# Retention over a prompt of 512 frames: one pass over all pairs of blocks, or blocks of 128 frames joined by carried states

## The chip, the core and the metric

The kernel runs on one core of a Trainium2 chip. A core has a matrix engine (TensorE, in the profile PE, its weight loads PEld), a vector engine (VectorE, DVE), a scalar engine (ScalarE, ACT), a general engine (GpSimd, POOL) and a queue engine (SyncE, SP), which run side by side and wait for each other by semaphores. DMA queues are fed here by SP (loads) and POOL (stores). The metric is the time of one execution on the device in microseconds, as the median of several runs.

## The reference

One inference step of an encoder layer with weights shared by a prompt (one sequence of 512 frames) and eight sample streams of 16 frames, at width 1024. The layer has a half-step feed-forward block, a mixer, a second feed-forward block and a per-layer embedding. The mixer projects the normed input once into all its parts and runs two token mixers: forgetting attention (FoX, 8 heads) and retention (4 heads with keys of 128 and values of 256). The part that matters here is the retention:

```python
def step(state, qkv):
    qc, kc, vc = ...                      # one chunk of 64 frames
    inter = einsum('bchk,bhkv->bchv', qc, state) * inter_decay
    att = einsum('bihk,bjhk->bhij', qc, kc) * intra_decay[None]
    intra = einsum('bhij,bjhv->bihv', att, vc)
    new_state = state * chunk_decay + einsum('bjhk,bjhv->bhkv', kc * kv_decay, vc)
    return new_state, (inter + intra)
```

Inside a chunk of 64 frames every frame sees every other, with decay gamma to the power |t - s|; earlier chunks are seen with decay gamma to the power (t - s), later ones not at all. The four heads have gamma = 1 - 2^-5 to 1 - 2^-8. The final state of the prompt and of the samples are outputs too. After the retention come an RMS norm of each head, a gate silu(rg) and a projection.

## The kernel before

All tokens stand in one axis of T = 640 columns: the prompt's 512 (S) and the samples' 128. Channels lie on the 128 partitions. Large products are made in fp32r with operands split into two parts (`wh`, `wl` of the weights; a high and a low part of x), three matmuls for one. The small products of attention and retention are plain fp32 matmuls, which show in the profile as two passes each.

The stage of interest is in the middle. The input projection is a list of units (`units`, from line 1552 on), each a weight load, splits of the weights, some 50 to 100 matmuls and a take of the result. They are run by a generator, `feed`. The retention's work is woven into it by hand: after each step of a head, `fill(FILL_R)` lets the feed issue matmuls worth 2.45 us by a planned clock (`clock`, counted up in `mm`). A scheduler that simulates the engines then orders each engine's instructions by this order and by when their operands are ready, so it can pull feed matmuls ahead or push a step back. After the last head `drain` issues what is left of the feed. What follows is the retention's output projection, whose operand is read back from `retd`.

A head (`Retention`, line 1325) goes through thirteen steps before the change:

- `rotate(0)`, `rotate(1)`: rotary embedding of k and q (DVE), from tiles loaded out of `zdram` by `first_loads` and `loads`.
- `scores(0)` to `scores(3)`: keys of block j (128 frames) against all queries from block j on, so 512, 384, 256 and 128 columns. Each goes to a PSUM bank of its own, and DVE multiplies it with the mask row of the head (`self.mask`, 128 x 512, loaded for each head into an `att` buffer), giving four `att` tiles. `scores(4)` is the samples' part.
- `values(0)`, `values(1)`: for each half of the 256 value channels, four matmuls of 512, 384, 256 and 128 columns added up in one bank, copied out by ACT. `square` squares them; `values_s` does the samples.
- `flip`: the keys transposed by PE; DVE scales each of the four blocks with the decay to the end of the prompt (`kd`), and the samples' block twice (`kb`).
- `sizes` (mean squares and their inverse roots, a row of small DVE instructions) and `gates` (two loads from `zdram`, silu on ACT).
- `state_p`: four matmuls of 256 columns add up the prompt's final state in one bank; ACT copies it and POOL stores it.
- `finish`: the norm's factors are spread by PE, DVE multiplies, POOL stores two tiles to `retd`.
- `states`: the samples' states, in four banks, added by DVE, stored by POOL (1 MB).

The next head's loads are issued at fixed steps: `first_loads` (k, q) at step 3, `loads` (the rest, v and the mask) at step 9, `more_loads` (the samples' state) at step 13. Three of a head's tiles (k and q; q's turned half with v; the samples' state) are taken in turn from four `kv` buffers, so a head's k and q go into the buffer of the state of two heads earlier, once that is stored. The `att` tag has 8 buffers, the `pa` tag 6 PSUM banks.

Line 205 is the matmul in `mm`, line 228 the transpose, lines 282 and 283 the split of weights; lines 816 to 834 take the results of feed units, line 1531 those of the FoX projection, which is the last of the feed.

Of the kernel before, what the change touches and what calls it, by code (L numbers as in the profile page):

```python
# [14 lines left out]
ALU = mybir.AluOpType  # L15
# [4 lines left out]
P = 128  # L20
D = 1024
KC = D // P
S = 512
NB = 8
# [26 lines left out]
for _name, _n in (  # L51
    ("ident", 128), ("triu", 128), ("trib", 128), ("tris", 128), ("causal", 128), ("bd", 128),
    ("sel8", 128), ("fold", 64), ("lmask", 16), ("cmask", 16), ("bsel", 8), ("kd", 16), ("ksd", 8),
):
    SM[_name] = (_at, _at + _n)
    _at += _n
# [7 lines left out]
def shape_constants():  # L64
# [25 lines left out]
    kd = np.zeros((P, RH, S // P))  # L90
    ksd = np.zeros((P, RH, 2))
    for h in range(RH):
        for t in range(S // P):
            kd[:, h, t] = gam[h] ** (S - 1 - (t * P + i)) * scale
        for j in range(2):
            ksd[:, h, j] = np.where(b % 2 == j, gam[h] ** (L - 1.0 - l) * scale, 0.0)
    put("kd", kd.reshape(P, -1))
    put("ksd", ksd.reshape(P, -1))

    q = np.arange(S)  # L100
    rmask = np.zeros((RH, P, S))
    smask = np.zeros((P, RH, P))
    gq = np.zeros((P, RH, 2, 2 * L))
    for h in range(RH):
        dist = q[None, :] - i[:, None]
        same = (q[None, :] // CHUNK) == (i[:, None] // CHUNK)
# [25 lines left out]
def kernel(  # L132
# [1192 lines left out]
    class Retention:  # L1325
# [33 lines left out]
        def scores(self, j):  # L1359
            kr, qr = self.z[0][0], self.z[1][0]  # L1360
            if j == 0:
                self.ats = []
            ps = bank()
            if j < 4:
                n = S - j * P
                mm(ps[:, :n], kr[:, j * P:(j + 1) * P], qr[:, j * P:S], True, True)
                at = att()
                nc.vector.tensor_tensor(at[:, :n], ps[:, :n], self.mask[:, :n], op=ALU.mult)
                self.ats.append(at)
            else:  # L1370
                mm(ps[:, :P], kr[:, S:], qr[:, S:], True, True)
                self.at_s, self.qg = tmp([P, P]), tmp([P, NB // 2, 2, 2 * L])
                nc.vector.tensor_tensor(self.at_s, ps[:, :P], smt[:, self.hd, :], op=ALU.mult)
                qp = qr[:, S:].rearrange("p (r m) -> p r m", r=NB // 2).unsqueeze(2).to_broadcast([P, NB // 2, 2, 2 * L])
                gp = gqt[:, self.hd].unsqueeze(1).to_broadcast([P, NB // 2, 2, 2 * L])
                nc.vector.tensor_tensor(self.qg, qp, gp, op=ALU.mult)

        def values(self, dvb):
# [4 lines left out]
            for j in range(4):  # L1383
                mm(po[:, j * P:S], self.vs[j][:, dsl], self.ats[j][:, :S - j * P], j == 0, j == 3)
# [32 lines left out]
        def flip(self):  # L1417
# [5 lines left out]
            for t in range(4):  # L1423
                nc.vector.tensor_scalar(self.kd[:, t, :], pk[:, t * P:(t + 1) * P], cs["kd"][:, hd * 4 + t:hd * 4 + t + 1], None, op0=ALU.mult)
# [24 lines left out]

        def state_p(self):  # L1450
            ps = bank()
            for t in range(4):
                mm(ps[:, :DV], self.kd[:, t, :], self.vs[t], t == 0, t == 3)
            sf = tmp([P, DV])
            nc.scalar.copy(sf, ps[:, :DV])
            nc.gpsimd.dma_start(o_state_p[0, 0, self.hd], sf)
# [167 lines left out]
    load(smt, c_smask)  # L1624
    heads = [Retention(hd) for hd in range(RH)]
# [144 lines left out]
```

## Time and profile before

| what | value |
|---|---|
| median of 3 runs (lowest, highest) | 1656.47 us (1654.16, 1657.26) |
| the profiled execution | 1657.02 us |
| its span, first to last instruction | 1655.3 us |
| granted TensorE clock, share of full speed | 0.999 |
| DMA, mean over the span | 150 GB/s, 248.66 MB |

A row of a view that groups instructions reads: line, engine, operation, tile written <- tiles read, shapes, count, then busy time in us, mean ns of one, and the idle time of the engine before them with what ended it. A row of a timeline reads: start in us, length in us, engine, line, operation, tiles, shapes and how many in a row. The view of stretches gives, for each stretch, each engine's busy time in us, the granted clock, the busy share of the DMA engines and GB/s. A wait "PE pa L205 <- DVE blk L1447: 1.9, 1, 1.9" says that matmuls into `pa` waited for that DVE line 1.9 us in all, once, at most 1.9.

### The profile page before, as it was taken

The numbers are of one execution on the slowest core, as the hardware profiler recorded it, in microseconds if no ns is written. First come the engines' busy times: TensorE is split into PE (matmuls) and PEld (weight loads), VectorE is DVE, ScalarE is ACT, GpSimd is POOL, SyncE is SP. The second block draws the span as 40 slices with busy tenths as digits, with TensorE's granted clock in tenths as the row PEclk, the third lists the DMA queues.
The fourth block names the chain that finished last, engine by engine and source line by source line (L and its number), as shares of the span: only waits on it lengthen the run. The fifth ranks groups of instructions, "written<-read, shape, count | busy, mean of one in ns | idle before, by whom it ended". The sixth has DMA issues, their size and how long they took to land.

```text
span 1655.3 us, 30447 instructions
## 1 busy us (share of the span) xinstructions
PE 1638.0 (99%) x12019; PEld 1562.2 (94%) x12019; DVE 1164.5 (70%) x2480; ACT 737.0 (45%) x1522; POOL 99.2 (6%) x180
## 2 busy tenths in 40 slices
PE   8999999999999999999999999999999999999998
PEld 8999999999999888888789988999999999999998
DVE  6884787586876646666688876658885687568663
ACT  6552344244454445344444345435553355235432
POOL 0000000000111111000001020001000000000000
PEclk9999999999999999999999999999999999999999
DMA  8244233433623225576765687634334424332531
GB/s 244 77 138 145 87 92 119 154 85 108 212 77 117 96 103 179 211 268 231 279 214 188 205 292 247 216 109 156 97 96 155 132 77 134 132 116 87 171 120 46
DMA packets 207647, 248.66 MB, mean 150 GB/s; under 512 B 10464, under 2 KB 176272, under 8 KB 203408
## 3 DMA queue, kind: packets, MB, share of 16 engines
q1 hardware_dynamic: 195264, 203.22, 38.4%
q0 software_dynamic: 12032, 43.42, 7.1%
q8 instruction: 94, 1.54, 0.4%
q14 instruction: 49, 0.40, 0.1%
q10 hardware_dynamic: 208, 0.08, 0.0%
HBM read 198.04 MB, written 48.65 MB: 149 GB/s over the span
## 4 chain that ended last, share of the span: by engine, by line
PE 84%; issue 9%; DMA 4%; DVE 2%; POOL 1%; ACT 1%; SPq 1%; POOLq 0%; DVEq 0%; ACTq 0%
PE pa L205 67%; PE pg L205 14%; PE pa L228 3%; DMA raw<-in_ffn_w_in_dram 2%; DMA blk<-zdram 1%; DVE wl L283 0%; DMA out_dram<-kv 0%; POOL zdram L832 0%; PE pg L228 0%; POOL zdram L835 0%; DMA kv<-in_x_prompt_dram 0%; SPq L650 0%; DMA kv<-zdram 0%; DVE raw L424 0%; DVE blk L283 0%
## 5 line engine op out<-in xcount | busy, mean ns | idle before, releaser
L282 ACT CAST wh<-raw 128x512 fp32r<-128x512 f32 (+1 forms) x525 | 316.1, 613 | 489.3 <-PE pa L205 296.8
L205 PE MATMUL pa<-blk,wh 128*128 128x320 f32 x2344 | 511.3, 311 | 2.9 <-ACT wh L282 1.0
L283 DVE TENSOR_TENSOR wl<-raw,wh 128x512 fp32r<-128x512 f32 (+1 forms) x525 | 351.8, 678 | 96.6 <-ACT wh L282 92.9
L205 PEld LDWEIGHTS pa<-blk,wh 128*128 128x128 f32 x2344 | 387.3, 188 | 10.9 <-ACT wh L282 2.4
L205 PE MATMUL pa<-blk,wl 128*128 128x320 f32 x1172 | 342.6, 308 | 0.0
L205 PE MATMUL pa<-kv,wh 128*128 128x320 f32 x1344 | 251.7, 308 | 0.0
L205 PEld LDWEIGHTS pa<-blk,wl 128*128 128x128 f32 x1172 | 215.4, 188 | 0.1
L205 PEld LDWEIGHTS pa<-kv,wh 128*128 128x128 f32 x1344 | 210.7, 188 | 0.0
L205 PE MATMUL pg<-blk,wh 128*128 128x320 f32 x768 | 177.0, 317 | 4.2 <-DVE pg L822 1.6
L205 PE MATMUL pa<-blk,blk 128*128 128x320 f32 (+2 forms) x1064 | 168.8, 304 | 0.0
L205 PE MATMUL pa<-kv,wl 128*128 128x320 f32 x672 | 154.6, 308 | 0.0
L205 PEld LDWEIGHTS pa<-blk,blk 128*128 128x128 f32 (+1 forms) x1064 | 151.8, 183 | 2.1 <-PE pa L205 1.2
L205 PE MATMUL pg<-wh,blk 128*128 128x256 f32 x768 | 148.2, 286 | 0.0
L205 PEld LDWEIGHTS pg<-blk,wh 128*128 128x128 f32 x768 | 127.4, 188 | 10.1 <-issue 2.5
L205 PEld LDWEIGHTS pg<-wh,blk 128*128 128x128 f32 x768 | 120.8, 188 | 6.1 <-issue 4.8
L205 PE MATMUL pg<-blk,wl 128*128 128x320 f32 x384 | 118.9, 310 | 0.0
L205 PEld LDWEIGHTS pa<-kv,wl 128*128 128x128 f32 x672 | 112.7, 188 | 0.0
L205 PE MATMUL pg<-wl,blk 128*128 128x256 f32 x384 | 108.4, 283 | 0.0
L283 DVE TENSOR_TENSOR blk<-raw,blk 128x512 fp32r<-128x512 f32 x82 | 56.3, 688 | 50.0 <-ACT blk L282 37.2
L282 ACT CAST blk<-raw 128x512 fp32r<-128x512 f32 x82 | 50.7, 621 | 79.2 <-DMA raw<-in_ffn_w_in_dram 65.6
L205 PE MATMUL pa<-wh,blk 128*128 128x256 f32 (+1 forms) x432 | 82.6, 285 | 0.0
L205 PEld LDWEIGHTS pg<-wl,blk 128*128 128x128 f32 x384 | 72.1, 188 | 1.7 <-issue 1.1
(289 smaller groups left out, 2247.7 us busy)
## 6 DMA issues: line engine op xcount, KB each, us to landing
raw<-in_ffn_w_in_dram SPq DMA_DIRECT2D x86, 512.0 KB, 5.2
raw<-in_w_in_mix_dram SPq DMA_DIRECT2D x25, 1024.0 KB, 5.5
raw<-in_ffn_w_out_dram SPq DMA_DIRECT2D x16, 1024.0 KB, 5.4
kv<-in_cache_fox_k_dram SPq DMA_DIRECT2D x16, 1024.0 KB, 6.4
kv<-in_cache_fox_v_dram SPq DMA_DIRECT2D x16, 1024.0 KB, 6.7
blk<-xd SPq DMA_DIRECT2D x48, 320.0 KB, 6.0
xd<-blk POOLq DMA_DIRECT2D x40, 320.0 KB, 3.2
zdram<-blk POOLq DMA_DIRECT2D x32, 320.0 KB, 2.8
```

Source lines behind the costliest of these rows:

```text
L205: i = nc.tensor.matmul(out, lhsT, rhs, start=start, stop=stop, **kw)
L228: tick(nc.tensor.transpose(out, in_, ident[: in_.shape[0], : in_.shape[0]]), 0.11)
L282: nc.scalar.copy(hi, src)
L283: nc.vector.tensor_tensor(lo, src, hi, op=ALU.subtract)
```

## The change

The four blocks of 128 frames become chunks of their own. Each block's scores are made against its own queries alone (four matmuls of 128 columns into one bank), masked by one DVE multiply with a 128 x 128 mask that all blocks share. The state behind each block is made before the values: `kd` now decays to the end of the block, one factor for all blocks, and `states_p` forms state t = state t-1 x gamma^128 + product of block t on DVE; two products share a bank. The last of these states is the prompt's final state and is stored from there, so `state_p` is gone. The queries of blocks 1 to 3 are scaled by gamma^(i+1) (`qd`), and `values` adds, for these blocks, state t-1 times `qd` to the product within the block.

The masks of all heads are two tiles of 128 x 512 (`masks`: within a block, and gamma^(i+1)), loaded once ahead of the heads into `att` buffers that stay taken. The steps are put in a new order, twelve for a head: `flip` third, then `scores`, `scores_s`, `states_p`, the values, `sizes` and `gates`, `states`, `finish`. The next head's `first_loads` are still at step 3, `loads` at step 6, `more_loads` at step 11. `FILL_R` stays 2.45.

```diff
-    rmask = np.zeros((RH, P, S))
+    rmask = np.zeros((2, P, RH, P))
...
-        rmask[h] = np.where(same | (dist >= 0), gam[h] ** np.abs(dist), 0.0) * scale
+        rmask[0, :, h] = np.where(same | (dist >= 0), gam[h] ** np.abs(dist), 0.0) * scale
+        rmask[1, :, h] = gam[h] ** (i[None, :] + 1.0)
...
-            self.mask = blk([P, S], tag="att")
-            load(self.mask, c_rmask[hd], 40.0)
...
-        def scores(self, j):
+        def scores(self):
...
+            for t in range(4):
+                sl = slice(t * P, (t + 1) * P)
+                mm(ps[:, sl], kr[:, sl], qr[:, sl], True, True)
+            self.at = att(shape=(P, 4, P))
+            within = masks[0][:, self.hd].unsqueeze(1).to_broadcast([P, 4, P])
+            nc.vector.tensor_tensor(self.at, ps.rearrange("p (t q) -> p t q", t=4), within, op=ALU.mult)
+            self.qd = att(shape=(P, 3, P))
+            fall = masks[1][:, self.hd].unsqueeze(1).to_broadcast([P, 3, P])
+            nc.vector.tensor_tensor(self.qd, qr[:, P:S].rearrange("p (t q) -> p t q", t=3), fall, op=ALU.mult)
...
+        def states_p(self):
+
+            held = [att(shape=(P, 2, DV)) for _ in range(2)]
+            self.behind = [held[t // 2][:, t % 2, :] for t in range(4)]
+            for u in range(2):
+                ps = bank()
+                for t in (2 * u, 2 * u + 1):
+                    new, st = ps[:, (t % 2) * DV:(t % 2 + 1) * DV], self.behind[t]
+                    mm(new, self.kd[:, t, :], self.vs[t], True, True)
+                    if t == 0:
+                        nc.vector.tensor_copy(st, new)
+                    else:
+                        nc.vector.scalar_tensor_tensor(st, self.behind[t - 1], gam[self.hd] ** P, new, op0=ALU.mult, op1=ALU.add)
+            nc.gpsimd.dma_start(o_state_p[0, 0, self.hd], self.behind[3])
...
-            for j in range(4):
-                mm(po[:, j * P:S], self.vs[j][:, dsl], self.ats[j][:, :S - j * P], j == 0, j == 3)
+            for t in range(4):
+                mm(po[:, t * P:(t + 1) * P], self.vs[t][:, dsl], self.at[:, t, :], True, t == 0, skip_group_check=True)
+                if t > 0:
+                    mm(po[:, t * P:(t + 1) * P], self.behind[t - 1][:, dsl], self.qd[:, t - 1, :], False, True, skip_group_check=True)
...
-            for t in range(4):
-                nc.vector.tensor_scalar(self.kd[:, t, :], pk[:, t * P:(t + 1) * P], cs["kd"][:, hd * 4 + t:hd * 4 + t + 1], None, op0=ALU.mult)
+            nc.vector.tensor_scalar(self.kd, pk.rearrange("p (t k) -> p t k", t=4), cs["kd"][:, hd:hd + 1], None, op0=ALU.mult)
...
-        def state_p(self):
-            ps = bank()
-            for t in range(4):
-                mm(ps[:, :DV], self.kd[:, t, :], self.vs[t], t == 0, t == 3)
-            sf = tmp([P, DV])
-            nc.scalar.copy(sf, ps[:, :DV])
-            nc.gpsimd.dma_start(o_state_p[0, 0, self.hd], sf)
...
+    masks = [att(shape=(P, RH, P)) for _ in range(2)]
+    for n in range(2):
+        load(masks[n], c_rmask[n])
...
-            lambda: r.rotate(0), lambda: r.rotate(1), lambda: (r.scores(0), heads[hd + 1].first_loads() if hd + 1 < RH else None),
-            lambda: (r.scores(1), r.scores(2)),
-            lambda: (r.scores(3), r.scores(4)), lambda: r.values(0), lambda: (r.values(1), r.square()), lambda: r.values_s(),
-            lambda: (r.flip(), heads[hd + 1].loads() if hd + 1 < RH else None),
-            lambda: (r.sizes(), until(("rg", hd)), r.gates()), lambda: r.state_p(), lambda: r.finish(),
-            lambda: (r.states(), heads[hd + 1].more_loads() if hd + 1 < RH else None),
+            lambda: r.rotate(0), lambda: r.rotate(1), lambda: (r.flip(), heads[hd + 1].first_loads() if hd + 1 < RH else None),
+            lambda: r.scores(), lambda: r.scores_s(),
+            lambda: (r.states_p(), heads[hd + 1].loads() if hd + 1 < RH else None),
+            lambda: r.values(0), lambda: (r.values(1), r.square()), lambda: r.values_s(),
+            lambda: (r.sizes(), until(("rg", hd)), r.gates()),
+            lambda: (r.states(), heads[hd + 1].more_loads() if hd + 1 < RH else None), lambda: r.finish(),
```

More of the change, by code (lines that the diff above doesn't have):

```diff
@@ L89, in shape_constants @@
     scale = DK ** -0.5
-    kd = np.zeros((P, RH, S // P))
+    kd = np.zeros((P, RH))
     ksd = np.zeros((P, RH, 2))
     for h in range(RH):
-        for t in range(S // P):
-            kd[:, h, t] = gam[h] ** (S - 1 - (t * P + i)) * scale
+        kd[:, h] = gam[h] ** (P - 1.0 - i) * scale
         for j in range(2):
             ksd[:, h, j] = np.where(b % 2 == j, gam[h] ** (L - 1.0 - l) * scale, 0.0)
-    put("kd", kd.reshape(P, -1))
+    put("kd", kd)
     put("ksd", ksd.reshape(P, -1))
-    q = np.arange(S)
-    rmask = np.zeros((RH, P, S))
+    rmask = np.zeros((2, P, RH, P))
     smask = np.zeros((P, RH, P))
@@ new lines, in scores_s @@
+        def scores_s(self):
+            kr, qr = self.z[0][0], self.z[1][0]
+            ps = bank()
+            mm(ps[:, :P], kr[:, S:], qr[:, S:], True, True)
+            self.at_s, self.qg = tmp([P, P]), tmp([P, NB // 2, 2, 2 * L])
+            nc.vector.tensor_tensor(self.at_s, ps[:, :P], smt[:, self.hd, :], op=ALU.mult)
+            qp = qr[:, S:].rearrange("p (r m) -> p r m", r=NB // 2).unsqueeze(2).to_broadcast([P, NB // 2, 2, 2 * L])
+            gp = gqt[:, self.hd].unsqueeze(1).to_broadcast([P, NB // 2, 2, 2 * L])
+            nc.vector.tensor_tensor(self.qg, qp, gp, op=ALU.mult)
@@ new lines, in states_p @@
+        def states_p(self):
+            held = [att(shape=(P, 2, DV)) for _ in range(2)]
+            self.behind = [held[t // 2][:, t % 2, :] for t in range(4)]
+            for u in range(2):
+                ps = bank()
+                for t in (2 * u, 2 * u + 1):
[6 more added lines that the diff above has]
+            nc.gpsimd.dma_start(o_state_p[0, 0, self.hd], self.behind[3])
```

21 lines of the change are left out of this document (3 added, 18 removed).

## The prediction

> **What bounds the kernel now.** I read the page first, for the engine that is busy and for the chain that ended last, then stretches of the four heads, then what ended the waits in them.
>
> ```profile
> span 1655.3 us, 30447 instructions
> PE 1638.0 (99%) x12019; PEld 1562.2 (94%) x12019; DVE 1164.5 (70%) x2480; ACT 737.0 (45%) x1522; POOL 99.2 (6%) x180
> PE 84%; issue 9%; DMA 4%; DVE 2%; POOL 1%; ACT 1%; SPq 1%; POOLq 0%; DVEq 0%; ACTq 0%
> ```
>
> TensorE is busy for 99% of the span and is 84% of the chain. A microsecond of its work taken away is a microsecond of time, unless PE then waits for something. What could be waited for is read from the stage itself. The next fence is the table of stretches from each head's first score matmul to the next head's, and then the list of waits of PE over the same time.
>
> ```profile
> core 0: us, PE busy (x) PEld busy (x) DVE busy (x) ACT busy (x) POOL busy (x), PEclk, DMA share, GB/s
> 853.00:907.00 54.00, 54.00 (x362) 49.41 (x361) 47.53 (x103) 22.40 (x42) 5.50 (x11) 1.00 0.49 158
> 907.00:957.00 50.00, 49.31 (x330) 44.56 (x329) 42.97 (x97) 19.86 (x40) 5.16 (x9) 1.00 0.65 215
> 957.00:999.00 42.00, 38.49 (x267) 33.83 (x265) 28.38 (x72) 20.94 (x48) 8.52 (x15) 1.00 0.91 316
> 999.00:1039.00 40.00, 38.09 (x244) 32.76 (x245) 26.88 (x66) 23.48 (x36) 3.62 (x6) 1.00 0.68 234
> ```
>
> ```profile
> PE pa L205 <- DVE blk L1447: 1.9, 1, 1.9
> PE pg L205 <- DVE pg L822: 1.6, 1, 1.6
> PE pg L205 <- DVE blk L1531: 1.6, 1, 1.6
> PE pg L205 <- DVE blk L831: 0.7, 1, 0.7
> ```
>
> Two things are to be seen. In heads 0 and 1 PE never or hardly stops, but VectorE (DVE) is busy 47.53 of 54 and 42.97 of 50 us, 88% and 86%. In heads 2 and 3 PE stands still for 3.5 and 1.9 us, and all but 0.3 of the stage's 6.1 us of PE waits are ended by DVE. So PE sets the pace of this stage and DVE is the next in line. The DMA share reaches 0.91 in head 2.
>
> **The matmuls removed (the main term).** An fp32 matmul appears as two passes. Pieces in a timeline overlap at their ends, so I measure from one start to a later start and take off the fp32r feed matmuls in between. These are head 0's scores, its values (both halves of the channels), and eight passes of 128 columns in its finish:
>
> ```profile
> 852.81 2.32 PE L205 MATMUL pa<-kv 128*128 128x512 f32 x8
> 854.88 0.54 PE L205 MATMUL pg<-blk,wh 128*128 128x320 f32 x2
> 855.26 0.31 PE L205 MATMUL pg<-blk,wl 128*128 128x320 f32 x1
> 855.40 0.45 PE L205 MATMUL pg<-blk,wh 128*128 128x320 f32 x2
> 855.70 0.31 PE L205 MATMUL pg<-blk,wl 128*128 128x320 f32 x1
> ...
> 860.46 1.66 PE L205 MATMUL pa<-att,kv 128*128 128x512 f32 x4
> 861.66 0.75 PE L205 MATMUL pa<-blk,wh 128*128 128x320 f32 x2
> 862.25 2.97 PE L205 MATMUL pa<-att,kv 128*128 128x256 f32 x12
> 864.98 0.54 PE L205 MATMUL pg<-blk,wh 128*128 128x320 f32 x2
> 865.35 0.31 PE L205 MATMUL pg<-blk,wl 128*128 128x320 f32 x1
> ...
> 900.16 1.05 PE L205 MATMUL pa<-sm,ty 128*128 128x128 f32 x8
> 900.97 0.54 PE L205 MATMUL pg<-blk,wh 128*128 128x320 f32 x2
> 901.35 0.31 PE L205 MATMUL pg<-blk,wl 128*128 128x320 f32 x1
> ```
>
> - A feed matmul: three from 855.26 to 855.70, so 0.147 us.
> - Scores before: 852.81 to 855.26 is 2.45 us, less two feed matmuls 2.16 us. They stream 512 + 384 + 256 + 128 = 1280 columns in two passes.
> - Values before: 860.46 to 865.35 is 4.89 us, less four feed matmuls 4.30 us, twice the scores, as it must be.
> - A pass of 128 columns: 900.16 to 901.35 is 1.19 us, less two feed matmuls 0.90 us for eight, so 0.112 us each.
> - Scores after: 4 matmuls of 128 columns, 8 passes, 0.90 us. Values after: (4 + 3) matmuls for each of two halves, 28 passes, 3.14 us.
>
> Before 6.46, after 4.04 us: 2.42 us less in a head, **9.7 us in four heads**. The state's matmuls (`kd` against `vs`, four of 256 columns) keep number and shape; they only stop accumulating in one region. The sample's parts, the transposes and the finish are unchanged on PE.
>
> **VectorE and ScalarE.** DVE rows for the shapes removed and for the nearest ones to those added:
>
> ```profile
> L1368 DVE TENSOR_TENSOR att<-pa,att 128x512 f32<-128x512 f32 (+3 forms) x16 | 7.0, 480 | 0.0
> L1424 DVE TENSOR_SCALAR att<-pa,sm 128x128 f32<-128x128 f32 x16 | 4.6, 342 | 0.0
> L1468 DVE SCALAR_TENSOR_TENSOR kv<-kv,pa 128x512 f32<-128x512 f32 x16 | 10.1, 679 | 0.5 <-PE pa L205 0.5
> L1301 DVE COPY att<-pa 128x512 f32<-128x512 f32 x8 | 5.5, 685 | 0.6 <-PE pa L228 0.5
> L1445 DVE TENSOR_TENSOR blk<-blk,blk 128x512 f32<-128x512 f32 x8 | 5.4, 686 | 5.3 <-ACT blk L1434 5.3
> L1376 DVE TENSOR_TENSOR tmp<-kv,tmp 128x256 f32<-128x256 f32 x4 | 1.6, 412 | 0.0
> ...
> L1455 ACT COPY tmp<-pa 128x256 f32<-128x256 f32 x4 | 1.5, 364 | 0.7 <-PE pa L205 0.7
> ```
>
> Removed in a head: 4 x 480 + 4 x 342 ns = 3.29 us of DVE and one ACT copy of 0.36 us. Added: one masked multiply of 512 columns, 0.68 (as L1445; L1376 already reads broadcast operands, at no visible cost); `qd`, 384 columns, halfway between 412 and 686, 0.55; `kd` in one go, at least 0.69 (L1301), at most the 1.37 of today, taken as 342 plus 384 columns at the 1.07 ns a column between L1376 and L1445, 0.75; a copy of 256 columns, 685 - 274 = 0.41; three decay-and-add of 256 columns, 679 - 274 each, 1.22. Together 3.61 us: **0.3 us more DVE in a head, 1.3 us in all**. PE loses 2.4 us of own work in a head, and one step with its 2.45 us of feed moves out of each head (12 steps, not 13). On head 1's row, DVE then carries about 43.0 + 0.3 less the feed's share (2.45 x 0.86 = 2.1), 41.2 us, over 50 - 4.9 = 45 us: 91%. Since DVE ends nearly all of PE's waits here, I charge its 1.3 us in full, as time given back. Its other end is nothing, if the load still hides under PE.
>
> **Moves and queues.** `flip` goes from step 9 to step 3, so `kd` is ready three steps ahead of its use, and the kv buffer that holds k and q of this head comes free for the next head's second load (now issued at step 6, not 9). `states` goes ahead of `finish`, so the sample's state store leaves POOL's queue one step sooner, ahead of the two `retd` stores. That matters, because this chain of waits stands in the trace:
>
> ```profile
> 957.08 5.97 DMA out_dram<-kv
> ...
> 963.07 3.09 DMA kv<-zdram
> ...
> 966.28 0.09 DVE kv L1355
> ```
>
> Head 3's k and q wait for the store of head 1's state, DVE waits for them at the head of its queue, and PE for the DVE instruction behind (the 1.6 us at L822). Earlier stores and loads can shorten this; a shorter head brings the need for them earlier by about as much. I take nothing for it. The bound on the good side is all 6.1 us of PE's waits.
>
> The mask loads are these, one of 256 KB in each head:
>
> ```profile
> att<-in_c_rmask_dram SPq DMA_DIRECT2D x4, 256.0 KB, 7.3
> ```
>
> ```profile
> 825.56 7.14 SPq L214 DMA_DIRECT2D kv<-zdram  x6
> ```
>
> They become two, both ahead of head 0's loads in the program, so 512 KB less is moved. The two tiles stay in two of the 8 `att` buffers, but a head now takes 5 more and not 6. Queued on SP they can delay head 0's loads by about an issue each; the second row shows those loads going out from 825.56 us on, and head 0's scores come at 852.81, so I take nothing.
>
> At the end, 4 x 2.45 = 9.8 us of planned feed are left behind the last head, which `drain` then issues. Today feed and head 3 end together, so this remainder covers head 3's way through `retd` and back:
>
> ```profile
> 1036.63 1.96 PE pg L205 x12
> 1038.59 6.53 PE pa L205 x48
> ```
>
> **The sum.** -9.7 + 1.3 = -8.4 us against the profiled execution, 1657.0 us with its span of 1655.3. The median of the three runs shown is 1656.5, 0.5 lower; there the sum gives 1648.1, and I say **1648 us**.
>
> **Rivals.**
> - *The stage's waits go too.* The earlier state stores and loads end the waits of heads 2 and 3. Up to 6.1 us more, without the DVE charge: 1656.5 - 9.7 - 6.1 = 1640.7. For it: each wait there hangs on a late load or a late head. Against: loads fall due earlier too.
> - *DVE becomes the bound* in heads 0 to 2. If each head gives back another 1.2 us, half of what PE gained, 1656.5 - 9.7 + 1.3 + 3.6 = 1651.7. For it: 91% on average leaves little for bursts. Against: at 88% head 0 shows no wait at all.
> - *The head's own chain of dependences is the bound.* Flip, `kd`, states and values now follow one another, the feed runs out, and PE idles for all that it saved: 1656.5 - 8.4 + 8.4, again 1656.5. For it: PE already idles 5.4 us in heads 2 and 3. Against: the 9.8 us of feed kept back.
> - *Short passes cost their weight loads.* 24 passes become 36 in a head. If the 12 added loads didn't hide, at the row's 0.19 us,
>
> ```profile
> L205 PEld LDWEIGHTS pa<-sm,ty 128*128 128x128 f32 x32 | 4.0, 190 | 0.0
> ```
>
> that is 12 x 4 x 0.19 = 9.1 us, and the time 1656.5 - 8.4 + 9.1 = 1657. Against it: this row's loads belong to the very passes that came every 0.112 us, less than one load. [...]
> - *The two halves of a bank (the slower side).* `states_p` puts two products into one PSUM bank: the second matmul may have to wait until DVE has read the first. That is two round trips PE to DVE to PE in a head, eight in all, with the feed queued behind the waiting matmul on PE. At the longest PE wait on DVE above, 1.9 us, that costs 15.2 us: 1656.5 - 8.4 + 15.2 = 1663.3. It cancels the gain from 8.4 / 8 = 1.05 us a trip on. For it: DVE is 91% full, so the copy and the sum stand behind others. Against: feed matmuls can be put between. [...]
>
> **How the numbers follow.** Forecast 0.50 (its own range 1645.5 to 1650, DVE charged at nothing or double); waits go too 0.15; DVE the bound 0.18; own chain 0.09; weight loads 0.02; bank halves 0.06. The range takes in the first three, 0.83: 1640 to 1653.5. A difference of 0.2%, 3.3 us, is about what a measurement of this kernel tells from none. Faster by more: 0.50 + 0.15 + 0.18 = 0.83; within: 0.09 + 0.02 = 0.11; slower: 0.06.
>
> **What would show it.** In the changed kernel's timeline eight score passes of 128 columns should take 0.9 us, and 28 value passes 3.1 us; if a pass comes at 0.19 us or more, the weight loads rule. PE busy should fall by 9 to 10 us over the whole span. In the list of waits of the stage, a `pa` matmul that waits for the new copy or sum on DVE would speak for the bank halves, and DVE busy over 95% of the heads' stretches for DVE as bound. PE idle between head 3's end and the branch matmuls would speak for the head's own chain. If PE busy falls by 10 and the span by far less, the forecast is wrong.

## The result, and the profile after

| | before | after |
|---|---|---|
| median of 6 runs each (lowest, highest) | 1656.51 us (1654.16, 1657.49) | 1646.83 us (1645.90, 1648.36) |
| profiled execution | 1657.02 us | 1648.36 us |
| its span | 1655.3 us | 1646.6 us |

The ratio of after to before is 0.9944, with an interval of 0.9932 to 0.9957: 9.7 us less by the medians, 8.7 us by the two profiled executions.

From the page of the changed kernel: busy times, and the engines' shares of the chain that ended last.

```profile
PE 1631.5 (99%) x12067; PEld 1562.8 (95%) x12067; DVE 1165.6 (71%) x2476; ACT 734.6 (45%) x1516; POOL 98.9 (6%) x180
PE 92%; DVE 3%; DMA 3%; ACT 1%; issue 1%; SPq 0%; DVEq 0%; ACTq 0%
```

PE is the bound as before. It issues 48 matmul passes more, 12 in each head, and is busy for 6.5 us less (1638.0 to 1631.5), though the prediction expected 9 to 10. So some 3 us of what the matmuls should save have come back as other busy time of PE, and the span fell by more than PE's busy time. Both need an explanation.

The four heads of the changed kernel, each from its first score matmul to the next head's; the columns are those of the view of stretches above.

```profile
851.00:900.00 49.00, 49.00 (x345) 45.22 (x344) 43.62 (x95) 19.62 (x37) 5.23 (x9) 1.00 0.56 179
900.00:950.00 50.00, 45.74 (x312) 42.12 (x312) 40.81 (x89) 17.61 (x37) 5.31 (x10) 0.97 0.63 212
950.00:990.00 40.00, 40.00 (x307) 37.83 (x306) 36.05 (x85) 21.35 (x51) 7.98 (x15) 1.00 0.78 264
990.00:1033.00 43.00, 41.80 (x297) 38.42 (x295) 26.49 (x65) 22.61 (x35) 4.06 (x8) 1.00 0.66 250
```

What ended PE's waits there:

```profile
PE pg L204 <- DVE blk L833: 2.7, 2, 2.3
PE pg L204 <- DVE blk L1541: 1.2, 1, 1.2
PE pg L204 <- DVE blk L830: 1.2, 1, 1.2
PE pa L204 <- DVE att L1390: 0.4, 1, 0.4
```

The waits are moved, not gone. Head 2 now has none, head 1 has 4.3 us of them, and 0.97 as its granted clock. All but 0.4 us are feed matmuls (`pg`) that wait for a bank to be taken by DVE. Only the last row is the new state copy (line 1390). DVE is busy for 89, 82 and 90% of heads 0 to 2, below the 95% that the prediction set as the sign of DVE as the bound.

The removed matmuls, in PE's timeline of the changed kernel: head 0's values, then its scores.

```profile
862.48 0.60 PE L204 MATMUL pa<-att,kv 128*128 128x128 f32 x4
...
864.04 0.39 PE L204 MATMUL pa<-att,kv 128*128 128x128 f32 x2
864.26 1.17 PE L204 MATMUL pa<-kv,tmp 128*128 128x256 f32 x10
...
851.31 0.60 PE L204 MATMUL pa<-kv 128*128 128x128 f32 x4
851.67 0.54 PE L204 MATMUL pg<-blk,wh 128*128 128x320 f32 x2
852.05 0.61 PE L204 MATMUL pa<-kv 128*128 128x128 f32 x4
852.42 0.40 PE L204 MATMUL pg<-blk,wl 128*128 128x320 f32 x1
852.65 0.45 PE L204 MATMUL pg<-blk,wh 128*128 128x320 f32 x2
```

From 862.48 to 864.26 there are sixteen passes of values and nothing else (between the rows shown 2, 6 and 2), in 1.78 us, 0.111 us each. The scores: 851.31 to 852.65 less three feed matmuls of 0.147 us, 0.90 us. Both are as predicted. The loss is elsewhere.

**Where the stage's time went.** To compare kernels whose instructions are ordered differently, I cut the stage at the same work: from the 3600th to the 4800th large fp32r matmul that PE issues, counted from the start. These two rows of the view of stretches are before and after:

```profile
794.48:1069.52 275.04, 268.92 (x1973) 240.60 (x1972) 207.84 (x458) 125.66 (x244) 28.71 (x49) 1.00 0.69 234
```

```profile
792.43:1062.41 269.98, 264.51 (x2021) 242.93 (x2020) 208.37 (x454) 121.11 (x238) 28.56 (x49) 0.99 0.68 237
```

The stage is 5.1 us shorter, and it already begins 2.05 us earlier. Within it I split the time by the kind of each PE instruction, from its start to the next one's: (a) retention's plain fp32 matmuls of 128 rows and columns, (b) the samples' matmuls that use a strip of 32 rows or 32 columns of the array, with what it takes to go into such a run and out of it, (c) PE's waits, (d) what else is longer than the same instruction usually takes. Part of (d) is passes at half the granted clock (0.50 in the view of stretches): such a stretch lasted 3.4 us in the first profile of after (944.1 to 947.5) and 6.8 us in that of feed_even (1037.3 to 1044.1), as the last section shows. In the second profile of after the clock stays at 1.00 from 939 to 948 us, and its (d) is 1.66 us lower. The rest, 200.15 us of feed and other small matmuls, is the same in all kernels. The labels are those of the experiments below; norm_first and wide_table run PE in the order of after, so that with its own two there are four profiles of it.

| kernel | stage, us | (a) plain | (b) strips | runs of strips | (c) waits | (d) other |
|---|---|---|---|---|---|---|
| before | 275.04 | 40.24 | 26.20 | 24 | 6.12 | 2.34 |
| before, a second profile | 276.00 | 40.24 | 26.19 | 24 | 4.10 | 5.32 |
| after | 269.98 | 30.35 | 29.74 | 31 | 5.47 | 4.27 |
| after, a second profile | 269.45 | 30.35 | 29.74 | 31 | 6.61 | 2.61 |
| old_math_new_order | 276.91 | 40.24 | 31.21 | 32 | 2.55 | 2.76 |
| finish_first | 277.24 | 30.35 | 28.15 | 26 | 12.88 | 5.71 |
| feed_even | 278.88 | 30.35 | 24.67 | 23 | 13.16 | 10.55 |
| packed_first | 270.90 | 30.35 | 25.56 | 22 | 9.66 | 5.19 |
| less_dve | 270.74 | 30.35 | 27.80 | 27 | 8.21 | 4.23 |
| within_only | 261.47 | 25.02 | 29.50 | 32 | 3.86 | 2.94 |
| products_first | 267.19 | 30.35 | 28.90 | 30 | 5.01 | 2.78 |
| products_less_feed | 269.48 | 30.35 | 26.52 | 26 | 7.68 | 4.79 |
| norm_first | 270.82 | 30.35 | 29.74 | 31 | 7.78 | 2.80 |
| wide_table | 270.75 | 30.35 | 29.74 | 31 | 5.96 | 4.55 |

Column (a) falls by 9.9 us, exactly the removed work. Of this 3.3 to 4.8 us come back (9.9 less 6.6, by the second profiles, or less 5.1), up to 5.7 us if norm_first and wide_table are counted in, and 3.5 of it stands in (b): the same strip matmuls, but in 31 runs and not 24. Strips and slow passes count as busy, so in the stage PE's busy time fell by only 4.4 us (268.92 to 264.51): the 9.9 less 3.5 in (b) and 1.9 in (d). The other 2.1 us of the 6.5 lie outside the stage. In head 0 the state update of the samples shows it. Before, sixteen of them ran in one piece:

```profile
902.98 1.15 PE L205 MATMUL pa<-kv,tmp 32*128 32x256 f32 x16
904.05 0.41 PE L205 MATMUL pg<-blk,wl 128*128 128x320 f32 x1
904.30 0.45 PE L205 MATMUL pg<-blk,wh 128*128 128x320 f32 x2
```

After, they come in two, with feed in between:

```profile
885.35 0.71 PE L204 MATMUL pa<-kv,tmp 32*128 32x256 f32 x6
885.99 0.56 PE L204 MATMUL pg<-blk,wh 128*128 128x320 f32 x2
886.39 0.31 PE L204 MATMUL pg<-blk,wl 128*128 128x320 f32 x1
...
887.95 1.12 PE L204 MATMUL pa<-kv,tmp 32*128 32x256 f32 x10
889.00 0.56 PE L204 MATMUL pa<-blk,wh 128*128 128x320 f32 x2
889.40 0.30 PE L204 MATMUL pa<-blk,wl 128*128 128x320 f32 x1
```

Before: 902.98 to 904.30 less one feed matmul, 1.17 us. After: 885.35 to 886.39 and 887.95 to 889.40, each less two feed matmuls, 0.75 + 1.16 = 1.91 us.

### The profile page after: what moved, and what is told of

It reads as the page before. It is cut to its first block, busy times and chain, and to the rows that moved or that the text cites. A ratio compares the mean times of both kernels' runs of the same rounds, so it can differ in the third digit from the quotient of the medians.

```text
span 1646.6 us, 30526 instructions
## 1 busy us (share of the span) xinstructions
PE 1631.5 (99%) x12067; PEld 1562.8 (95%) x12067; DVE 1165.6 (71%) x2476; ACT 734.6 (45%) x1516; POOL 98.9 (6%) x180
## 4 chain that ended last, share of the span: by engine, by line
PE 92%; DVE 3%; DMA 3%; ACT 1%; issue 1%; SPq 0%; DVEq 0%; ACTq 0%
PE pa L204 70%; PE pg L204 18%; PE pa L227 4%; DMA raw<-in_ffn_w_in_dram 2%; DVE wl L282 1%; DMA kv<-zdram 1%; DMA blk<-zdram 0%; ACT tmp L532 0%; ACT wh L281 0%; PE pg L227 0%; DVE raw L433 0%; DMA kv<-in_x_prompt_dram 0%; ACT blk L281 0%; ACT L1452 0%; DVE raw L422 0%
```

## The experiments

Each ratio is to the kernel before, run beside it on the same chip (medians 1654.3 to 1654.9 us there). The theory at the outset: PE work sets the time, and part of the saving is given back because DVE is nearly full. The rivals: the order of dependent steps holds the heads; the state products' shared banks do; the feed kept back does.

**after_again**, the changed kernel as it is, for a second profile and a second chip.

> The changed kernel, unaltered. In its first profile three things stand beside the 9.7 us of matmul work taken away: the first 41 us of the span were 2.1 us shorter than before, though nothing there is touched but a constants table 12 columns narrower; the retention stage was only 5.1 us shorter; and 1.1 us came from the last 300 us. Theory A (the start is chance, the arrival of the first loads): the start comes out anywhere between 38 and 42 us here, the stage again about 205 us, and the time 1645 to 1650 us. Theory B (the narrower table makes the start faster): the start is 38.9 us again to 0.3 us. Ratio to the kernel before by either: 0.993 to 0.9965.

Measured: 1646.57 us, ratio 0.9952 (0.9939 to 0.9964), 8.0 us less than the kernel before on that chip (1654.58). The two chips' ratios agree within their intervals; the gain is 8 to 10 us. The 300th large matmul comes at 61.7 us, against 61.4 in the first profile and 63.5 in that of before: the earlier start is there again.

**within_only** takes 48 more passes of values off PE (two halves of three blocks are six matmuls in a head, two passes each). It leaves out what the earlier blocks add to the values.

```diff
-                mm(po[:, t * P:(t + 1) * P], self.vs[t][:, dsl], self.at[:, t, :], True, t == 0, skip_group_check=True)
-                if t > 0:
-                    mm(po[:, t * P:(t + 1) * P], self.behind[t - 1][:, dsl], self.qd[:, t - 1, :], False, True, skip_group_check=True)
+                mm(po[:, t * P:(t + 1) * P], self.vs[t][:, dsl], self.at[:, t, :], True, True, skip_group_check=True)
```

> The changed kernel without the matmuls that bring in the earlier blocks' states in the values: 6 matmuls, 12 passes of 128 columns, are left out in each head, 48 passes in all; the states themselves are still made. Theory A (PE's work is the time, one for one, at 0.112 us a pass): 5.4 us less than the changed kernel, 1641.5 us, ratio about 0.991. Rival (the head's own chain or DVE sets the stage's end): PE idles instead, and the time falls by less than 2 us.

Measured: 1639.52 us, 0.9912 (0.9897 to 0.9927), 7.05 us less than after_again. Column (a) falls by 5.33 us, the stage by 8.0 to 8.5. PE work pays at least one for one. The surplus stands in (c) and (d), 6.8 us here and 9.2 to 9.7 after. The likely reason is that the values no longer hang on the states; this run takes away work and dependence at once and can't tell them apart.

**packed_first** gives the strip matmuls of `values_s` and `states` precedence, so that they stay in one run.

```diff
-            for j in range(2):
-                for pr in range(NB // 2):
-                    mm(po[pr * 32:(pr + 1) * 32, :DV], self.qg[:, pr, j, :], self.st[:, 2 * pr + j, :], False, j == 1, skip_group_check=True)
+            with tc.high_priority():
+                for j in range(2):
+                    for pr in range(NB // 2):
+                        mm(po[pr * 32:(pr + 1) * 32, :DV], self.qg[:, pr, j, :], self.st[:, 2 * pr + j, :], False, j == 1, skip_group_check=True)
...
+            with tc.high_priority():
+                for j in range(2):
+                    for r in range(NB // 2):
...
```

> The samples' packed matmuls (32 columns or 32 rows of the array each, in values_s and states) are put ahead of the feed in the scheduler's order, so that a run of them isn't broken up. In the changed kernel's first profile they stood in 22 runs with 18.5 us in all, before the change in 15 runs with 15.0 us; entering and leaving a run costs about 0.4 us. Theory A (the broken runs ate 3.5 us of the gain): runs fall to 15 or fewer and the time falls by 2 to 4 us below the changed kernel, ratio about 0.992. Rival (they sit in time that PE would have waited anyway): runs fall, waits of PE rise by as much, and the time stays within 1 us of the changed kernel.

Measured: 1648.7 us, 0.9964 (0.9951 to 0.9976). The runs fall from 31 to 22 and column (b) by 4.2 us, but (c) and (d) rise from some 9.5 to 14.9. The intervals overlap, so it is no faster, and probably 2 us slower. PE now stands where it had issued feed, above all at the row of the norm (PE's waits in this kernel's stage):

```profile
PE pa L204 <- DVE ty L345: 5.5, 3, 3.2
```

So the broken runs are not the cause of the loss by themselves. They are the cheaper of two forms of it: at these places PE has to wait for a dependent step, or turn to the feed and back.

**less_dve** moves two DVE instructions of each head, the scaling of `kd` and the first state copy, to ACT.

```diff
-                        nc.vector.tensor_copy(st, new)
+                        nc.scalar.copy(st, new)
...
-            nc.vector.tensor_scalar(self.kd, pk.rearrange("p (t k) -> p t k", t=4), cs["kd"][:, hd:hd + 1], None, op0=ALU.mult)
+            nc.scalar.activation(self.kd, pk.rearrange("p (t k) -> p t k", t=4), AF.Copy, scale=cs["kd"][:, hd:hd + 1])
```

> The changed kernel with two of DVE's new pieces given to ACT: the scaling of kd (512 columns) and the copy of the first state (256 columns), 1.1 us of DVE in a head, 4.4 us in all. In the stage the work taken away is 9.9 us, yet it is only 5.1 to 5.6 us shorter: waits, broken runs of packed matmuls and other gaps took the rest. Theory A (crowded DVE is what holds PE up there): the stage, 269.5 to 270 us from the 3600th to the 4800th feed matmul, falls by 2 us or more, the time to 1644.5 us or less. Rival (the order of dependent steps in a head holds it up, whoever does them): the stage stays within 1.5 us.

Measured: 1649.44 us, 0.9970 (0.9959 to 0.9981). Its stage, in the view of stretches:

```profile
792.65:1063.39 270.74, 262.53 (x2021) 241.36 (x2020) 204.81 (x444) 122.44 (x244) 28.68 (x49) 1.00 0.67 235
```

DVE is busy for 3.6 us less than in the changed kernel (204.81 against 208.37), and the stage isn't shorter (270.74 against 269.98 and 269.45). The time of the whole is rather longer than the changed kernel's. The two pieces take no longer on ACT (0.69 and 0.37 us, against 0.75 and 0.42 on DVE), so it isn't that the chain got longer by them. So DVE's load is not what gives the time back.

**old_math_new_order**: the arithmetic of before, in the twelve-step order of the change.

```diff
-            lambda: r.rotate(0), lambda: r.rotate(1), lambda: (r.scores(0), heads[hd + 1].first_loads() if hd + 1 < RH else None),
-            lambda: (r.scores(1), r.scores(2)),
-            lambda: (r.scores(3), r.scores(4)), lambda: r.values(0), lambda: (r.values(1), r.square()), lambda: r.values_s(),
...
+            lambda: r.rotate(0), lambda: r.rotate(1), lambda: (r.flip(), heads[hd + 1].first_loads() if hd + 1 < RH else None),
+            lambda: (r.scores(0), r.scores(1), r.scores(2), r.scores(3)), lambda: r.scores(4),
+            lambda: (r.state_p(), heads[hd + 1].loads() if hd + 1 < RH else None),
...
```

> The arithmetic of the kernel before (wide scores and values, masks loaded for each head, one state matmul group) in the twelve steps of the changed order, with the four scores in one step and state_p at step 6. Theory A (the gain is the matmul work taken away): PE's work is that of before, and the time is 1653 to 1658 us, ratio 0.998 to 1.002. Rival (the order, with earlier stores and 9.8 us of feed kept for the end, is what gained): ratio 0.997 or lower, and the stage at least 3 us shorter than before.

Measured: 1657.99 us, 1.0023 (1.0013 to 1.0032). The order alone gains nothing; it costs some 3 us. In the stage it trades 3.6 us of (c) and (d) (8.9 on the mean of the two profiles of before, 5.3 here) for 5.0 us more of (b), 32 runs. So the broken runs come with the order, not with the arithmetic.

**before_again**, the kernel before, one run, for its second profile.

> The kernel before, unaltered, for a second profile of it. In the five profiles of changed kernels so far the first 300 feed matmuls were over 1.1 to 2.1 us sooner than in the one profile of before (63.5 us), and the stretch from 1474 to 1520 us of before was 2.0 to 2.1 us shorter, though nothing in either place is changed. Theory A (chance of one execution): the second profile of before shows one or both of them gone, that is the 300th feed matmul at 61.4 to 62.5 us, and that stretch at 43.8 us in place of 45.9. Theory B (a lasting effect of the change outside its stage, by the narrower constants table or another order of instructions): both stand as in the first profile, 63.5 us and 45.9 us.

Measured: 1656.78 us (one run, so no interval). Each theory holds in one place. The 300th large matmul comes at 63.7 us, as late as in the first profile (63.5), so the later start is lasting. The stretch from 1474 to 1520 us is 2.0 us shorter than in the first profile, as it is in every other profile, so there the first one was slow by chance. Columns (a) and (b) repeat to 0.01 us, while (c) and (d) differ by 2 and 3 us between the two profiles of one kernel: a microsecond of a single stage's total is chance.

**finish_first** swaps the last two steps of the change back: the norm's finish ahead of the samples' states.

```diff
-            lambda: (r.states(), heads[hd + 1].more_loads() if hd + 1 < RH else None), lambda: r.finish(),
+            lambda: r.finish(), lambda: (r.states(), heads[hd + 1].more_loads() if hd + 1 < RH else None),
```

> The changed kernel with finish again ahead of states, as before the change; still twelve steps. Theory A (the state's store one step sooner frees the kv buffer sooner, and the samples' state work covers the wait for the norm's small DVE instructions): the time rises by 1 to 4 us, with a wait of PE on the small DVE lines or of DVE on the k and q loads. Rival (this swap does nothing): within 1 us of the changed kernel.

Measured: 1658.59 us, 1.0019 (1.0009 to 1.0029): the whole gain of 8 to 10 us is lost, 12 us by the medians where 1 to 4 were expected. Its longest waits of PE in the stage:

```profile
PE pa L204 <- DVE ty L345: 4.6, 2, 3.4
PE pg L204 <- DVE blk L827: 4.3, 1, 4.3
```

Line 345 is the last of the small DVE instructions of the norm (`rsqrt_mean`), whose result `finish` spreads by PE. With `states` between them, PE has strip matmuls to do while that row runs; without, it waits 4.6 us for it. The other long wait, 4.3 us, is a feed bank that DVE has not yet taken. The profiled run, 1655.1 us, was near the fastest of the ten timed, so the typical loss is larger than this trace shows.

**norm_first** gives that row of small instructions precedence.

```diff
-            sums = tiny(TB)
-            nc.vector.tensor_copy(sums[:, :4], pm[:, :4])
...
+            with tc.high_priority():
+                sums = tiny(TB)
+                nc.vector.tensor_copy(sums[:, :4], pm[:, :4])
...
```

> The changed kernel with the norm's row of small DVE instructions in sizes ahead of all other DVE work in the scheduler's order. With finish ahead of states the time had risen by 12 us, and PE waited 4.6 us on these instructions. Theory A (the head's own chain, of which this row is the longest piece, 7 to 13 us from the sums to the spread factors, holds the stage up): the row shrinks to 5 us or less, waits and gaps fall, and the stage is 2 us or more shorter than 269.5 us. Rival (in the changed order states covers this row): within 1.5 us, or longer, as the feed's DVE work is pushed back.

Measured: 1647.22 us, 0.9952 (0.9936 to 0.9969), no different from the changed kernel. But the time from the last `sums` matmul to the first spread stayed as it was (9.3, 12.5, 7.0, 11.7 us in heads 0 to 3, against 9.3, 13.5, 7.0, 11.7): the precedence had hardly anything to move. Its stage, 270.8 us, is within 1.5 us, as the rival had it, but the run says nothing on how much the row costs.

**feed_even** spends the feed that the change keeps back: twelve fills of 2.65 instead of thirteen of 2.45.

```diff
-FILL_P0, FILL_P1, FILL_S0, FILL_S, FILL_R, FILL_B = 1.76, 1.6, 19.8, 10.0, 2.45, 6.4
+FILL_P0, FILL_P1, FILL_S0, FILL_S, FILL_R, FILL_B = 1.76, 1.6, 19.8, 10.0, 2.65, 6.4
```

> The changed kernel with 2.65 us of feed after each step in place of 2.45, so that twelve steps carry as much feed (31.8 us) as thirteen did before. Theory A (denser heads crowd DVE, the feed's splits come late, and broken runs and waits follow): DVE's share in heads 0 and 1 goes back towards 87%, and the time falls by 1 to 3 us. Rival (the density doesn't matter, the order of the feed is chance): within 1 us either way.

Measured: 1656.74 us, 1.0013 (1.0004 to 1.0022). Again the whole gain is lost; neither expectation had this. The end of head 3, in PE's timeline (in brackets the wait ahead of an instruction, and what ended it):

```profile
1031.20 0.30 PE L204 MATMUL pg<-blk,wl 128*128 128x320 f32 x1
1031.44 1.15 PE L204 MATMUL pa<-kv,tmp 32*128 32x256 f32 x16
1038.13 2.05 PE L204 MATMUL pa<-sm,ty 128*128 128x128 f32 x8 [5.55 <-DVE ty L345]
```

The last feed matmul is out at 1031.20, the states follow, and then PE has nothing until the norm is there.

**products_first** issues both products of a bank before DVE reads either, so the second matmul is no longer put behind the read of the first half. One such wait, 0.4 us on line 1390, stands in the changed kernel's list, none in this run's.

```diff
+                news = [ps[:, e * DV:(e + 1) * DV] for e in range(2)]
+                for e in range(2):
+                    mm(news[e], self.kd[:, 2 * u + e, :], self.vs[2 * u + e], True, True)
                 for t in (2 * u, 2 * u + 1):
-                    new, st = ps[:, (t % 2) * DV:(t % 2 + 1) * DV], self.behind[t]
-                    mm(new, self.kd[:, t, :], self.vs[t], True, True)
+                    new, st = news[t % 2], self.behind[t]
```

> The changed kernel with the two products of a bank in states_p issued one after the other, ahead of DVE's copy and sum, so that the second doesn't wait until DVE has read the first. Theory A (feed matmuls fill those round trips; one wait of 0.4 us on that copy stands in the first profile): within 1 us of the changed kernel, ratio 0.9945 to 0.9955. Rival (the trips lengthen a head's chain and so hold up the stage): 2 us or more below the changed kernel, ratio 0.9935 or lower.

Measured: 1644.66 us, 0.9939 (0.9923 to 0.9956), the fastest of the kernels that do all the work, and between the two expectations. Its stage:

```profile
792.66:1059.85 267.19, 262.18 (x2021) 240.85 (x2020) 209.28 (x454) 119.32 (x236) 28.54 (x49) 1.00 0.69 239
```

That is 2.3 and 2.8 us less than the two profiles of the changed kernel. The medians differ by 1.9 us from after_again, but by the first result's ratio (0.9944) it is only 0.8 us, and the intervals overlap: a small gain that is likely but not shown.

**products_less_feed** holds still more feed back in that version, `FILL_R` 2.25.

> The changed kernel with the two products of a bank issued one after the other (the best so far, 1644.7 us, stage 267.2 us), and 2.25 us of feed after each step in place of 2.45, so that another 9.6 us of planned feed are kept for the end. With 2.65 the feed ran out ahead of head 3, PE waited 5.6 us on its norm, and the time rose by 10 us. Theory A (feed has to be left for the last head's end and no more): with 2.45 that is already so, and 2.25 stays within 1.5 us of 1644.7 us. Rival 1 (each us kept pays on): 1643 us or less. Rival 2 (denser heads wait more within): 1647 us or more, with more waits on DVE in heads 0 to 2.

Measured: 1647.42 us, 0.9960 (0.9947 to 0.9974), no gain over products_first and probably 2.8 us slower. Waits and other gaps rise from 7.8 to 12.5 us: what is kept for the end is missing within the heads. Of the three values tried (2.65 in feed_even) 2.45 is the best.

**wide_table** pads the small constants' table to its old width. The change had cut `kd` from 16 columns to 4, and the table from 1024 columns to 1012.

```diff
-    ("sel8", 128), ("fold", 64), ("lmask", 16), ("cmask", 16), ("bsel", 8), ("kd", 4), ("ksd", 8),
+    ("sel8", 128), ("fold", 64), ("lmask", 16), ("cmask", 16), ("bsel", 8), ("kd", 4), ("ksd", 8), ("pad", 12),
```

> The changed kernel with the table of small constants padded from 1012 back to 1024 columns; nothing reads the pad. The 300th feed matmul came at 63.4 to 63.7 us in the three profiles of kernels with the table of 1024 columns, and at 61.4 to 62.4 us in the seven with 1012. Theory A (the table's row pitch of 4096 bytes slows the first loads): 63.2 us or later here, and a time about 1.7 us above the changed kernel. Theory B (chance, or something else of the change): 61.4 to 62.4 us.

Measured: 1650.15 us in one run, beside 1654.89 for the kernel before, so no interval. What it tells is the start. The table's load among the first issues, and a first weight load at 100 us, on SP's queue: before,

```profile
12.01 2.25 SPq L650 DMA_DIRECT2D raw<-in_ffn_w_in_dram  x2
14.30 2.47 SPq L671 DMA_DIRECT2D sm<-in_c_small_dram  x1
...
98.71 0.37 SPq L265 DMA_DIRECT2D raw<-in_ffn_w_out_dram  x1
```

after,

```profile
11.13 2.00 SPq L649 DMA_DIRECT2D raw<-in_ffn_w_in_dram  x2
13.17 2.16 SPq L670 DMA_DIRECT2D sm<-in_c_small_dram  x1
...
96.78 0.37 SPq L264 DMA_DIRECT2D raw<-in_ffn_w_out_dram  x1
```

and with the padded table.

```profile
14.16 2.46 SPq L670 DMA_DIRECT2D sm<-in_c_small_dram  x1
...
98.35 0.37 SPq L264 DMA_DIRECT2D raw<-in_ffn_w_out_dram  x1
```

In all four profiles with 1024 columns the table's issue takes 2.46 to 2.47 us, in all ten with 1012 columns 2.16. The 300th large matmul starts at 63.2 to 63.7 us in the four, at 61.4 to 62.4 in the ten. So the narrower table brings 0.8 to 2.3 us, far from the stage, and padding it takes them away again. Why is open: the issues ahead of the table's are shorter as well (2.00 and 2.25 us in the first rows), and no run tried other widths.

## Why the prediction came out as it did

The forecast, 1648 us, lies 1.2 us from the median of 1646.83, and its chain of reasons holds in the main: PE is the bound, and removed matmuls are removed time. But two of its terms were off, in opposite directions.

1. *The matmuls removed (-9.7 us).* Right. Measured -9.9 us (40.24 to 30.35), at 0.111 us a pass. That removed PE work pays at least one for one, within_only shows (5.33 us removed, 7.05 gained).
2. *"Short passes cost their weight loads."* Out: the sixteen passes came every 0.111 us, each with a weight load of 0.19 us (12 of 191 ns and 4 of 192), and the time is 10 us under the 1657 of this rival.
3. *"I charge its 1.3 us in full, as time given back."* Here the step failed, in size and in place. The durations were right: in the changed kernel's groups the new DVE instructions are these (mean ns of one in the second number after the bar):

```profile
L1442 DVE TENSOR_SCALAR att<-pa,sm 128x512 f32<-128x512 f32 x4 | 3.0, 745 | 0.2 <-PE pa L227 0.2
L1365 DVE TENSOR_TENSOR att<-pa,att 128x512 f32<-128x512 f32 x4 | 2.7, 682 | 0.0
L1368 DVE TENSOR_TENSOR att<-kv,att 128x384 f32<-128x384 f32 x4 | 2.2, 546 | 0.0
L1390 DVE COPY att<-pa 128x256 f32<-128x256 f32 x4 | 1.7, 415 | 0.0
L1392 DVE SCALAR_TENSOR_TENSOR att<-att,pa 128x256 f32<-128x256 f32 x12 | 4.9, 412 | 0.0
```

   Together 3.62 us a head where 3.61 was worked out. But 3.3 to 5.7 us were given back, by the profiles that one compares, not 1.3, and not to DVE's load: taking 3.6 us off DVE (less_dve) gave nothing, so *DVE becomes the bound* is out as well. What is left is the order of dependent steps in a head, in two parts by the table of the stage; each part rests on one or two profiles, so a microsecond of it can be chance. The new order alone costs 1.4 us (276.9 against 275.5, the mean of the two profiles of before; 3 us by the medians of the whole), by breaking the strip matmuls. And at the same order the heads with less PE work wait more: (c) and (d) go from 5.3 to 9.2 or 9.7, with (b) 1.5 us lower, so 2.4 to 3.0 us. Of this within_only and products_first take some 2.5 us back, both by easing the states' chain, which makes it the likely place; that is argued. The rival that *the waits go too* (1640.7) failed on the same ground.
4. *Moves and queues: "I take nothing for it."* The net was small, but each move was worth the whole change. `states` ahead of `finish` holds 11 us (finish_first against after_again: ratios 1.0019 and 0.9952), in part because the strip matmuls cover the norm's row. The prediction looked only at POOL's queue there. The feed left for the end, 9.8 us by the plan, holds 10 us (feed_even); that it "covers head 3's way" was right, and the nearest cover needed is the norm's row, before `retd`.
5. *"The head's own chain of dependences is the bound"* (1656.5) and *"the two halves of a bank"* (1663.3). The first is not what happened, but it is what happens without the feed kept back: 1656.74. The second is small: at most some 2 us over eight trips, 0.24 us each by the medians (products_first), against the 1.05 us from which it would have cancelled the gain. In the list of waits above only 0.4 us hang on the new copy.
6. *What the prediction left out.* All of it was looked for in the stage. The narrower table of constants starts the kernel 0.8 to 2.3 us earlier, and the profile of after has 2.05 of this. Against the profiled execution: -9.9 + 4.8 - 2.05 = -7.1 us to the end of the stage. The other 1.6 us lie behind it, where both kernels do the same work: mainly 1.1 us more at about 1370 us and 2.1 less between 1474 and 1520. Both are chance of single executions. The 2.1 us are those of before's first profile, which is alone in them: its second and all profiles of other kernels take 2.0 to 2.1 us less there. The 1.1 stand in after's first profile and, with 0.9, in before's second, and in no other (0.4 at most).

So the number was good partly by luck: a give-back that was 2 us or more too small and a gain of about 2 us at the start that was missing nearly cancelled.

## What to carry to other kernels

Here, where TensorE is busy for 99% of the span, removed matmul passes were worth their time at least one for one (5.33 us removed and 7.05 gained in within_only), before what the new order of steps gives back, and the pace of the nearest passes in the trace priced them well (0.112 us a pass before, 0.111 after). What is given back is not read from another engine's load: find the row of small dependent instructions in each step, and ask what PE does in the meantime, for that cover (here the next step's matmuls, and feed kept for the end) can be worth the whole gain (8 to 10 us here, lost in finish_first and in feed_even). Compare two traces from the k-th matmul to the n-th of work that both share, and split by kind; then a gain at the kernel's start isn't taken for one of the stage.

## What the runs showed of the hardware

**Half the granted clock behind a wait of 2.31 us.** In the changed kernel PE waits for 2.31 us, and 0.95 us after it starts again, at 944.08, its matmuls slow down; eight passes of 128 columns take 1.71 us from start to start (945.65 to 947.36) instead of some 0.9 us:

```profile
943.13 0.53 PE L204 MATMUL pg<-blk,wh 128*128 128x320 f32 x2 [2.31 <-DVE blk L833]
...
945.65 1.91 PE L204 MATMUL pa<-sm,ty 128*128 128x128 f32 x8
947.36 0.45 PE L227 MATMUL pa<-sm,tmp 128*128 128x128 f32 x2
```

The granted clock of these stretches is the number after the five engines:

```profile
944.50:946.00 1.50, 1.50 (x8) 1.50 (x7) 0.43 (x2) 0.33 (x1) 0.00 (x0) 0.50 1.03 415
946.00:947.50 1.50, 1.50 (x9) 1.50 (x8) 0.69 (x1) 0.61 (x2) 0.00 (x0) 0.50 1.06 323
947.50:949.00 1.50, 1.50 (x13) 1.50 (x12) 1.40 (x3) 0.00 (x0) 0.00 (x0) 1.00 0.98 321
```

The clock was 0.50 for 3.4 us, from 944.1 to 947.5. In the second profile of the same kernel a wait of 2.15 us left it at 1.00 (939 to 948 us); in the second profile of before, whose longest wait in the heads is 2.1 us, it was 0.50 from 969 to 971 us. So the length of the wait alone doesn't decide. In the first profile of before the clock stayed at 1.00 from 15.6 to 1654 us, behind waits of up to 1.9 us, but was 0.50 from 12.2 to 15.6, behind waits of 1.53 and 0.72 us that ended at 10.71 and 12.13. Across that stretch its lag behind the first profile of after, whose clock was 1.00 there, grew from 0.96 us (12.13 against 11.17) to 2.55 (15.58 against 13.03).

Three longer waits each came with a half clock. In finish_first, behind those of 3.4 and 4.3 us, the clock was 0.64 and 0.51 over 942 to 944 and 944 to 946 us, and 0.51 and 0.64 over 963 to 965 and 965 to 967, each 3.4 us at 0.50. Around feed_even's wait of 5.55 us, which ended at 1038.13, the half clock lasted twice as long, from 1037.3 to 1044.1: the clock was 0.94 over 1032.5 to 1038, then 0.50, and 0.97 over 1044 to 1046.

```profile
1042.00:1044.00 2.00, 2.00 (x9) 2.00 (x9) 1.37 (x2) 0.00 (x0) 1.09 (x2) 0.50 0.41 164
1044.00:1046.00 2.00, 2.00 (x15) 2.00 (x14) 0.00 (x0) 0.47 (x1) 0.00 (x0) 0.97 0.60 200
```

**Turning between whole-array and strip matmuls cost 0.5 us a run.** Seven more runs of the same strip matmuls cost 3.5 us (column (b), before and after); in head 0 above one more run cost 0.74 us. Over the whole table column (b) goes from 24.67 us in 23 runs to 31.21 in 32.
